# More two by two steps in a fp32 residual block: three up pairs of the second FFN phase and one more gate block

## The chip, the cores and the metric

The kernel runs on one core of a Trainium2 chip. The metric is the device time of one execution in microseconds (us). It is taken in several runs, and one more execution is recorded by the hardware profiler; the page of the profile, its trace and the time of that execution belong together.

## The reference

One residual block on x of 512 tokens by 1024 features, in fp32:

```
h    = rms_norm(x, g1);  proj = h @ w_in          # conv B, C, in | q, k, v | f | gates a, b
y_c  = (B * causal_dwconv3(C * xin)) @ w_out_conv
y_a  = forgetting_attention(q, k, v, f) @ w_out_attn        # 8 heads of 64
x    = x + (sigmoid(ga) * y_c + sigmoid(gb) * y_a) @ w_o
h    = rms_norm(x, g2);  [a | b] = causal_dwconv3(h @ w_up) # 2 x 2816
x    = x + (silu(a) * b) @ w_down
out  = rms_norm(x, gf)
```

## The kernel before

Everything is held transposed: features on the partitions, the 512 tokens along the free axis. A weight block of 128 output features and all 1024 inputs is one chunk (512 KB); the list `stream` names all chunks in the order of use. For a chunk, SyncE (SP) loads `raw`, ScalarE (ACT) rounds it to its high half `wh` (L274), and VectorE (DVE) takes the low half `wl` = raw − wh (L278). Both halves are double buffered, the raws have four buffers (two more kinds for forms, below), and loads run up to seven chunks ahead. The activations are split in the same way (`x1h` and `x1l`, `gh` and `gl`), and a product is three passes: high·high, low·high, high·low (`mm3` L308, `passes` L326). So a chunk's `wl` is wanted by TensorE (PE) only for the last third of its matmuls.

**Two by two steps.** Some products are made in the Strassen-Winograd way: for two blocks of outputs, two of inputs and the two halves of the tokens, seven products take the place of eight. This needs sums of weight blocks and of activation blocks. The sums of weights ("forms") are made in DRAM by DMAs (`make_forms`): plain copies on SP's queue (`put`) and accumulating copies on GpSimd's (POOL) queue (`add`), paced by `slot()`. A double (two products of this kind side by side) comes as two chunks, P (the weights as they are, three blocks) and F (four sums). The sums of activations are made on DVE, by `x_sums` for the gates and by `up_forms` for the up projection; `seven` issues the products; their results are put together from four PSUM banks on DVE and ACT (`gate_pair`, `merge`, `combine`).

**Stages of before (us).** v 0 to 30; q and k to 53; attention with the rest of the input projection to 180; gates, the two branch outputs and their mix, block by block for j = 0 to 7, to 295 (gates from block `GJ` = 3 on in two by two steps); w_o to 339; FFN ups of phase 0 (pairs 0 to 11 of a and b blocks, pairs `SUP` = 1, 2, 5 in steps) to 468; `STEPS[0]`, their down projection in steps, to 525; ups of phase 1 (pairs 12 to 21, all plain) to 634; `STEPS[1]` to 670; a plain rest of the down projection and the final norm.

**What sets the order.** Engines run their instructions in program order. Behind each `split()` the program places small work from the list `later`, up to a budget in us for that chunk (`run_later`); `flush` and `flush_only` empty the list for given tags where a product wants the result. Work tagged "e" is that of the up pairs: `fz` (the PSUM block times the norm), `fu` (three taps of the convolution), then `glu`, which makes silu(a)·b of a pair (`ge`, `go`), and per two pairs q the sums of them (`go`) and the splits into `gh` and `gl`, the operands of the down projection. `HELD` = 2: the sums of output block 2 of the down projection stay in PSUM over phase 1; the others are added to x by `combine` after each phase (`cz`, `cu`).

Of the kernel before, what the change touches and what calls it, by code (L numbers as in the profile page):

```python
# [53 lines left out]
HELD = 2  # L54

GJ = 3
# [14 lines left out]
def block_kernel(ctx, tc, xT, vecs, wv, win, wmix, wo, wup, wst, wdp, outT):  # L71
# [118 lines left out]
    def make_forms(n0, n1, key):  # L190

        size, step, shift = GROUPS[key]
        make_forms.slot = 0
# [4 lines left out]
        for g, (a, b) in enumerate(zip(cuts, cuts[1:])):  # L198
# [15 lines left out]
            todo_bg.extend((make_forms.slot + step * k + shift * g, op) for k, op in enumerate(ops))  # L214
# [167 lines left out]
    ycl = abp.tile([P, 4, S], F32R, tag="ycl", name="ycl")  # L382

# [359 lines left out]

    fill = []
# [41 lines left out]
    def seven(doubles, n0, sets, operand, goes_on=None, stays=None, done=None, of="q"):  # L786
# [14 lines left out]
        for n, (name, prods) in enumerate(todo):  # L801
            wh, wl = chunk(name)
# [4 lines left out]
            for c, i, (xh, xl), b, h in prods:  # L807
                if i not in open_:
# [32 lines left out]
    def mt(name):  # L841
        return mp.tile([P, S], F32, tag="mt", name=name, bufs=6)
# [12 lines left out]
    for q in range(4):  # L855
        nc.gpsimd.dma_start(xt[:, 2 * q : 2 * q + 2, :], xT[:, 2 * q : 2 * q + 2, :])
    xq = xt.rearrange("p (q b) (h c) -> p q (b h) c", b=2, h=2)
    xqh, xql = (t.rearrange("p (q b) (h c) -> p q (b h) c", b=2, h=2) for t in (xth, xtl))

    def x_scale(q):  # L860
        def f():
            for kb in (2 * q, 2 * q + 1):
                nc.scalar.activation(xt[:, kb, :], xt[:, kb, :], AF.Copy, scale=col(G1 + kb))

        return f

    def x_sums(qs):
        b11, b12, b21, b22 = (xq[:, qs, i, :] for i in range(4))

        def f():  # L870
# [637 lines left out]
```

## Time and profile before

| what | value |
|---|---|
| median of 3 runs | 696.37 us (695.74 to 696.41) |
| the profiled execution | 695.75 us, span 693.9 us |
| busy: PE / DVE / ACT / POOL | 686.2 / 531.4 / 359.2 / 178.3 us |
| mean TensorE clock granted | 0.998 |

The span is the time between the first and the last recorded instruction; 1.85 us lie around it. Busy time of PE counts matmuls; weight loads (PEld) run beside them. A row of a timeline has start, duration, engine, line, operation, output<-inputs, and in brackets how long the engine was idle ahead of it and who released it. A row of a group has count, busy time in all, mean ns of one, and the idle time ahead of the group with its releasers. A DMA row has count, KB each and the median us from issue to landing.

### The profile page before, as it was taken

What the parts mean: (1) busy time and instruction counts of PE and PEld (TensorE: products, weight loads), DVE (VectorE), ACT (ScalarE), POOL (GpSimd) and SP (SyncE); (2) the same over time, 40 slices, a digit from 0 to 9 for tenths busy, and PEclk for the clock granted to TensorE, in tenths of its full rate; (3) what the DMA queues carried; (4) which work ended last, traced back from release to release, by engine and by line L of the source; (5) the groups of instructions that cost most, each with busy time, mean ns of one, the idle gap of its engine ahead of it and who ended that gap; (6) DMA issues with size and microseconds to landing.
All of it is one profiled execution on the core that took longest, in us unless ns stands there. A gap on an engine that the chain in (4) does not pass through costs nothing.

```text
span 693.9 us, 14635 instructions
## 1 busy us (share of the span) xinstructions
PE 686.2 (99%) x5972; PEld 684.6 (99%) x5972; DVE 531.4 (77%) x826; ACT 359.2 (52%) x565; POOL 178.3 (26%) x194
## 2 busy tenths in 40 slices
PE   9999999999999999999999999999999999999996
PEld 9999999999999999999999999999999999999996
DVE  6677877776577778768879799888774677777894
ACT  5665655644565444446554455545443344445572
POOL 4134846532221201113513134210000313222000
PEclk9999999999999999999999999999999999999999
DMA  7528988543698596766899776355646686776513
GB/s 256 158 70 272 197 200 193 129 91 92 223 263 244 166 269 193 207 217 141 114 316 294 201 178 135 116 177 176 201 128 232 141 195 157 188 169 172 164 31 122
DMA packets 58387, 124.68 MB, mean 180 GB/s; under 512 B 5280, under 2 KB 26800, under 8 KB 58320
## 3 DMA queue, kind: packets, MB, share of 16 engines
q1 hardware_dynamic: 40776, 99.68, 44.5%
q0 software_dynamic: 16304, 22.88, 20.9%
q10 hardware_dynamic: 1240, 1.19, 0.5%
q8 instruction: 47, 0.77, 0.4%
q14 instruction: 20, 0.16, 0.1%
HBM read 121.57 MB, written 39.32 MB: 232 GB/s over the span
## 4 chain that ended last, share of the span: by engine, by line
PE 96%; DVE 3%; issue 0%; ACT 0%; DVEq 0%
PE dn L326 24%; PE p_up L308 21%; PE p_in L308 14%; PE p_up L326 6%; PE p_wo L308 6%; PE yc L308 3%; PE ya L308 3%; PE pa L472 2%; PE pb L474 2%; PE p_q L308 2%; PE p_k L308 2%; PE p_gb L308 2%; PE p_ga L308 2%; PE o L653 2%; PE tp L636 1%; PE pdB L308 1%
## 5 line engine op out<-in xcount | busy, mean ns | idle before, releaser
L308 PE MATMUL p_up<-x1h,wh_up 128*128 128x256 f32 x464 | 90.5, 276 | 0.0
L308 PE MATMUL p_up<-x1h,wl_up 128*128 128x256 f32 x464 | 90.4, 276 | 0.0
L308 PE MATMUL p_up<-x1l,wh_up 128*128 128x256 f32 x464 | 90.3, 276 | 0.0
L308 PEld LDWEIGHTS p_up<-x1h,wh_up 128*128 128x128 f32 x464 | 69.9, 188 | 0.0
L308 PEld LDWEIGHTS p_up<-x1h,wl_up 128*128 128x128 f32 x464 | 69.9, 188 | 0.0
L308 PEld LDWEIGHTS p_up<-x1l,wh_up 128*128 128x128 f32 x464 | 69.8, 188 | 0.0
L274 ACT ACTIVATE wh_up<-raw_up 128x1024 fp32r<-128x1024 f32 x38 | 40.2, 1057 | 49.6 <-PE p_up L308 43.0
L210 POOL DMA_DIRECT2D f<-in_wst_dram x57 | 65.5, 1309 | 0.1
L278 DVE TENSOR_TENSOR wl_F<-raw_F,wh_F 128x1024 fp32r<-128x1024 f32 (+1 forms) x36 | 47.8, 1328 | 18.5 <-ACT wh_F L274 18.2
L308 PE MATMUL p_in<-xgh,wh_in 128*128 128x256 f32 x288 | 56.8, 279 | 0.0
L308 PE MATMUL p_in<-xgh,wl_in 128*128 128x256 f32 x288 | 56.6, 278 | 0.0
L308 PE MATMUL p_in<-xgl,wh_in 128*128 128x256 f32 x288 | 56.5, 278 | 0.0
L278 DVE TENSOR_TENSOR wl_up<-raw_up,wh_up 128x1024 fp32r<-128x1024 f32 x38 | 47.1, 1240 | 12.1 <-ACT wh_up L274 12.1
L274 ACT ACTIVATE wh_F<-raw_F 128x1024 fp32r<-128x1024 f32 (+1 forms) x36 | 37.9, 1053 | 35.4 <-PE dn L326 27.8
L1206 POOL TENSOR_TENSOR ge<-fu,fu 128x512 f32<-128x512 f32 x11 | 18.8, 1706 | 141.6 <-DVE fu L565 117.6
L274 ACT ACTIVATE wh_P<-raw_P 128x768 fp32r<-128x768 f32 (+1 forms) x36 | 30.0, 834 | 31.6 <-PE dn L326 22.3
L278 DVE TENSOR_TENSOR wl_P<-raw_P,wh_P 128x768 fp32r<-128x768 f32 (+1 forms) x36 | 35.0, 972 | 13.7 <-ACT wh_P L274 9.1
L308 PEld LDWEIGHTS p_in<-xgh,wh_in 128*128 128x128 f32 x288 | 44.7, 188 | 0.7
L326 PE MATMUL dn<-gl,wh_F 128*128 128x256 f32 x192 | 45.1, 276 | 0.0
L326 PE MATMUL dn<-gh,wh_F 128*128 128x256 f32 x192 | 45.1, 276 | 0.0
L308 PEld LDWEIGHTS p_in<-xgl,wh_in 128*128 128x128 f32 x288 | 43.7, 188 | 0.0
L308 PEld LDWEIGHTS p_in<-xgh,wl_in 128*128 128x128 f32 x288 | 43.6, 188 | 0.0
(349 smaller groups left out, 2148.5 us busy)
## 6 DMA issues: line engine op xcount, KB each, us to landing
raw_up<-in_wup_dram SPq DMA_DIRECT2D x38, 512.0 KB, 4.2
raw_F<-f SPq DMA_DIRECT2D x35, 512.0 KB, 4.5
raw_P<-in_wst_dram SPq DMA_DIRECT2D x35, 384.0 KB, 4.9
raw_in<-in_win_dram SPq DMA_DIRECT2D x26, 512.0 KB, 3.5
f<-in_wst_dram POOLq DMA_DIRECT2D x35, 256.0 KB, 6.4
f<-in_wst_dram SPq DMA_DIRECT2D x17, 512.0 KB, 5.7
f<-in_wst_dram POOLq DMA_DIRECT2D x17, 512.0 KB, 8.0
f<-f SPq DMA_DIRECT2D x34, 256.0 KB, 5.4
```

Source lines behind the costliest of these rows:

```text
L210: return lambda: keep(nc.gpsimd.dma_start(dst, src, accum_op=ALU.add))
L274: ins = nc.scalar.activation(hi, raw, AF.Copy)
L278: ins = nc.vector.tensor_sub(lo, raw, hi.bitcast(F32))
L308: keep(nc.tensor.matmul(out[:, cs], w, x[:, cs], start=start and i == 0 and c == 0, stop=stop and i == 2 and c == len(cut) - 1,))
L326: keep(nc.tensor.matmul(out, wl if x == 1 else wh, xl if x == 2 else xh, start=opens and bk not in seen, stop=closes and bk not in left,))
L472: keep(nc.tensor.matmul(pa[t][:, :VW], xt, w[:, VB:], start=start, stop=stop))
L474: keep(nc.tensor.matmul(pb[t], xt, w[:, :VB], start=start and t % 2 == 0, stop=stop and t % 2 == 1))
L636: keep(nc.tensor.transpose(tp[:, ks], pt[:, ks], ident))
L653: keep(nc.tensor.matmul(o[:, 2 * P * e + c0 : 2 * P * (e + 1)], w, x[:, kb, c0:], start=e == 0 and kb == 0 and i == 0, stop=e == 1 and kb ...
L1206: keep(nc.gpsimd.tensor_mul(ge, a.rearrange(halves_of, h=2), b.rearrange(halves_of, h=2)))
```

## The change

- `GJ` goes from 3 to 2: the gates of block 2 are made in steps. `SUP` becomes one tuple for each phase: up pairs 14, 16 and 18 of phase 1 are made in steps too, with forms of their own (`make_forms(..., "up1", 20)`).
- The activation sums of the up projection are needed in both phases. `up_forms(q, ph)` makes them in phase 0 in two buffers by turns (`y` in `gx` or `hp`), and writes each to DRAM (`ys`). In the operand slots 26 to 41 they stand for phase 0; for phase 1 they are read back from `ys` through one buffer `y`, each quarter after the split of the one before, and split into slots 0 to 15, which the down projection of phase 0 has used until then. The first load is issued ahead of `STEPS[0]`, the splits are due at its last chunk and the three after it.
- `HELD` goes: block 2's sums are added to x after both phases, and phase 1 has its PSUM banks. The list `later` is not emptied at the start of phase 1 except of "e" work.
- The x sums for the gates: the loads of `xt` and the scales and sums are moved out of the gate stage. The tile `xt` has memory from the start, so its four loads wait for nothing; the scales and sums are placed in attention. The gates' temporaries use the memory of `x1`, which is loaded in two pieces of 1 MB later.
- In `up`, behind the second block of a phase's last pair: where "e" work is pending, it is flushed, and one more `split()` follows.

The core of the diff (the code of `xt` is only moved, so its removal at the old place is left out):

```diff
@@ -51,20 +51,20 @@
 )
-HELD = 2
-GJ = 3
+GJ = 2
 GATES = tuple(((j, q), (j, q + 1)) for j in range(GJ, KB) for q in (0, 2))
 PLAIN = [(m, k) for m in (6, 7) for k in range(*PHASES[1])]
 PCUTS = (0, 8, 12, 20)
-SUP = (1, 2, 5)
-XF = 26
-UPD = tuple(((j, q), (j, q + 1)) for j in SUP for q in (0, 2))
-DOUBLES = GATES + UPD + STEPS[0] + STEPS[1]
-N0 = len(GATES) + len(UPD)
-GROUPS = {"gate": (2, 4, 1), "up": (2, 4, 1), 0: (2, 4, 1), 1: (2, 3, 1)}
+SUP = ((1, 2, 5), (14, 16, 18))
+XF = (26, 0)
+UPD = tuple(tuple(((j, q), (j, q + 1)) for j in js for q in (0, 2)) for js in SUP)
+DOUBLES = GATES + UPD[0] + STEPS[0] + UPD[1] + STEPS[1]
+NU = [len(GATES), len(GATES + UPD[0] + STEPS[0])]
+ND = [NU[i] + len(UPD[i]) for i in range(2)]
+GROUPS = {"gate": (2, 4, 1), "up0": (2, 4, 1), "up1": (2, 4, 1), 0: (2, 4, 1), 1: (2, 3, 1)}
@@ -187,10 +187,11 @@
-    def make_forms(n0, n1, key):
+    def make_forms(n0, n1, key, start=0):
         size, step, shift = GROUPS[key]
-        make_forms.slot = 0
+        if not start:
+            make_forms.slot = 0
         cuts = [n0]
@@ -211,7 +212,7 @@
             ops = (put(f0, x0), add(f0, x1), put(f1, f[:, :, :m]), add(f1, x1[:, :, m:]), put(f2, f1), add(f2, x2))
-            todo_bg.extend((make_forms.slot + step * k + shift * g, op) for k, op in enumerate(ops))
+            todo_bg.extend((start + step * k + shift * g, op) for k, op in enumerate(ops))
         todo_bg.sort(key=lambda w: w[0])
@@ -381,6 +382,10 @@
+    yg = ExitStack()
+    yp = yg.enter_context(tc.tile_pool(name="yp", bufs=1))
+    xt = yp.tile([P, KB, S], F32, tag="xt", name="xt")
     at = ExitStack()
@@ -740,6 +745,39 @@
     acc, bank_s, bank_t = ring(2, 0, 1), ring(3, 4), ring(5, 6)
+    for q in range(4):
+        nc.gpsimd.dma_start(xt[:, 2 * q : 2 * q + 2, :], xT[:, 2 * q : 2 * q + 2, :])
+    xq = xt.rearrange("p (q b) (h c) -> p q (b h) c", b=2, h=2)
+    def x_scale(q):
+        def f():
+            for kb in (2 * q, 2 * q + 1):
+                nc.scalar.activation(xt[:, kb, :], xt[:, kb, :], AF.Copy, scale=col(G1 + kb))
+        return f
+    def x_sums(qs):
+        b11, b12, b21, b22 = (xq[:, qs, i, :] for i in range(4))
+        def f():
+            nc.vector.tensor_sub(b11, b11, b12)
+            nc.vector.tensor_sub(b12, b22, b12)
+        def g():
+            nc.vector.scalar_tensor_tensor(b22, b11, -1.0, b22, op0=ALU.mult, op1=ALU.subtract)
+            nc.vector.scalar_tensor_tensor(b21, b22, -1.0, b21, op0=ALU.mult, op1=ALU.subtract)
+        return f, g
+    k = len(parts) + 2
+    for q in (0, 2):
+        f, g = x_sums(slice(q, q + 2))
+        for i in (q, q + 1):
+            later.append((k + i - q, 0, (("q", i),), x_scale(i)))
+        later.append((k + 2, 1.4, (("q", q),), f))
+        later.append((k + 3, 1.5, (("q", q),), g))
+        k += 4
@@ -799,6 +837,8 @@
         for n, (name, prods) in enumerate(todo):
+            if tick and name[0] == "P":
+                slot()
             wh, wl = chunk(name)
@@ -811,22 +851,23 @@
                     open_[i][b][:, th[h]], (i, b), wh[:, cs], wl[:, cs], xh, xl,
-                    (i, b) not in before and i != goes_on, (i, b) not in after and i != stays,
+                    (i, b) not in before, (i, b) not in after,
                 ))
             passes(out, len(out))
             if name[0] == "F":
                 for i in sorted({i for _, i, *_ in prods}):
-                    if (i, 0) not in after and i != stays:
+                    if (i, 0) not in after:
                         done(i, open_.pop(i), sets[i])
             split_next()
-    acc = ring(3, 4, 5, 6, 0, 1, 2, 7)
+    acc = ring(3, 4, 5, 6, 2, 7)
     xp = ctx.enter_context(tc.tile_pool(name="xp", bufs=1, side="right"))
-    xt = xp.tile([P, KB, S], F32, tag="x1", name="xt")
+    xm = xp.tile([P, KB, S], F32, tag="x1", name="xm")
     xth = xp.tile([P, KB, S], F32R, tag="x1h", name="xth")
     xtl = xp.tile([P, KB * S + PADR], F32R, tag="x1l", name="xtl")[:, : KB * S]
     xtl = xtl.rearrange("p (a b) -> p a b", b=S)
+    xqh, xql = (t.rearrange("p (q b) (h c) -> p q (b h) c", b=2, h=2) for t in (xth, xtl))
@@ -839,7 +880,10 @@
     def mt(name):
-        return mp.tile([P, S], F32, tag="mt", name=name, bufs=6)
+        mt.n += 1
+        return xm[:, (mt.n + 3) % KB, :]
+    mt.n = 0
@@ -884,16 +903,9 @@
-    k = [c[0] for c in stream].index("mix1")
-    for q in (0, 2):
-        f, g = x_sums(slice(q, q + 2))
-        for i in (q, q + 1):
-            later.append((k, 0, (("q", i),), x_scale(i)))
-        later.append((k, 1.4, (("q", q),), f))
-        later.append((k, 1.5, (("q", q),), g))
-        for i in (q, q + 1):
-            later.append((k + 1, 1.25, (("q", i),), x_split(i)))
-        k += 2
+    k = [c[0] for c in stream].index("mix0")
+    for q in range(4):
+        later.append((k + q // 2, 1.25, (("q", q),), x_split(q)))
@@ -943,15 +955,15 @@
-    make_forms(len(GATES), N0, "up")
+    make_forms(NU[0], ND[0], "up0")
     for j in range(KB):
         gs = []
         for _ in range(3):
             slot()
         if j == KB - 1:
-            x1 = xp.tile([P, KB, S], F32, tag="x1", name="x1")
-            for q in range(4):
-                nc.gpsimd.dma_start(x1[:, 2 * q : 2 * q + 2, :], xT[:, 2 * q : 2 * q + 2, :])
+            assert mt.n == 3 * KB
+            x1 = xm
+            nc.gpsimd.dma_start(x1[:, :4, :], xT[:, :4, :])
         if j == 0:
@@ -960,7 +972,7 @@
             if j == GJ:
-                acc = ring(2, 7, 3, 4)
+                acc = ring(3, 4, 2, 7)
             seven(GATES[2 * (j - GJ) : 2 * (j - GJ) + 2], 2 * (j - GJ), {j: (0, 1, 5, 6)}, gate_form, done=gate_pair(j, gs))
@@ -980,6 +992,8 @@
     mg.close()
+    nc.gpsimd.dma_start(x1[:, 4:, :], xT[:, 4:, :])
+    yg.close()
     ab.close()
@@ -1036,11 +1050,13 @@
-    def up_forms(q):
-        y = gx.tile([P, 4, 2 * P], F32, tag="y", name=f"y{q}")
+    ys = dr.tile([4, P, 4, 2 * P], F32, tag="ys", name="ys")
+    def up_forms(q, ph):
+        y = (gx if ph or q % 2 else hp).tile([P, 4, 2 * P], F32, tag="y", name=f"y{ph}{q}")
         b11, b12, b21, b22 = (y[:, i, :] for i in range(4))
-        fs = slice(XF + 4 * q, XF + 4 * q + 4)
+        fs = slice(XF[ph] + 4 * q, XF[ph] + 4 * q + 4)
@@ -1055,22 +1071,33 @@
         def parts_of():
             nc.scalar.activation(gh[:, fs, :], y, AF.Copy)
+            if not ph:
+                keep(nc.scalar.dma_start(ys[q], y))
             nc.vector.tensor_sub(gl[:, fs, :], y, gh.bitcast(F32)[:, fs, :])
+            if ph and q < 3:
+                up_forms(q + 1, ph)
+        if ph:
+            keep(nc.sync.dma_start(y, ys[q]))
+            due = [c[0] for c in stream].index(f"F{ND[0] + len(STEPS[0]) - 2}") + q
+            later.append((due, 0.85, (("x", q),), parts_of))
+            return
         for f, us in ((scale, 0.85), (sums, 0.85), (parts_of, 1.25)):
             later.append((0, us, (("x", q),), f))
-    def up_form(q, g):
+    def up_form(ph, q, g):
         if g < 3:
             kb, hs = (2 * q, 2 * q + 1, 2 * q + 1)[g], th[(0, 0, 1)[g]]
             return x1h[:, kb, hs], x1l[:, kb, hs]
-        n = XF + 4 * q + (0, 3, 1, 2)[g - 3]
+        n = XF[ph] + 4 * q + (0, 3, 1, 2)[g - 3]
         return gh[:, n, :], gl[:, n, :]
     po = None
-    make_forms(N0, N0 + len(STEPS[0]), 0)
+    make_forms(ND[0], ND[0] + len(STEPS[0]), 0)
+    make_forms(NU[1], ND[1], "up1", 20)
     for j in range(KB):
@@ -1105,11 +1132,11 @@
     acc = turns(0, 1, *(2, 3, 4, 5) * 2, 6, 7, 0, 1, 2, 3, 4, 5)
-    USETS = {1: (2, 3, 4, 5), 2: (6, 7, 0, 1), 5: (6, 7, 0, 1)}
+    USETS = dict.fromkeys(SUP[1], (2, 3, 4, 5)) | {1: (2, 3, 4, 5), 2: (6, 7, 0, 1), 5: (6, 7, 0, 1)}
     ssq3 = xp.tile([P, S], F32, tag="ssq", name="ssq3")
     def place(ph, q):
-        return (q - PHASES[ph][0] // 2) * (NF + ph)
+        return (16, 24, 32, 0, 8)[q - PHASES[1][0] // 2] if ph else q * NF
@@ -1134,6 +1161,9 @@
                 split_next()
+                if any(("e",) in w[2] for w in later):
+                    flush_only((("e",),))
+                    split()
             z = [None]
@@ -1292,10 +1322,8 @@
         if ph:
-            flush()
-            acc = turns(*X * 5)
-        if ph:
-            make_forms(N0 + len(STEPS[0]), len(DOUBLES), ph)
+            acc = turns(6, 7, 0, 1, 6, 7, 0, 1, 6, 7, 0, 1, 6, 7)
+            make_forms(ND[1], len(DOUBLES), ph)
         for j in range(j0, j1):
@@ -1309,14 +1337,15 @@
             up(j, ph, nrm["b"], pu)
+        if not ph:
+            up_forms(0, 1)
+        flush_only((("e",),))
+        seven(
+            STEPS[ph], ND[ph], ({0: X, 1: Y, 3: X, 2: Y}, {0: X, 1: Y, 2: Y})[ph],
+            lambda q, g: (gh[:, place(ph, q) + g, :], gl[:, place(ph, q) + g, :]),
+            done=lambda i, banks, ids: combine(ph, i, banks, ids), tick=True,
+        )
         assert not todo_bg
-        flush((("e",),))
-        seven(
-            STEPS[ph], N0 + ph * len(STEPS[0]), ({0: X, 1: Y, 3: X, 2: Y}, {0: X, 1: Y, 2: Y})[ph],
-            lambda q, g: (gh[:, place(ph, q) + g, :], gl[:, place(ph, q) + g, :]),
-            goes_on=HELD if ph == 1 else None, stays=HELD if ph == 0 else None,
-            done=lambda i, banks, ids: combine(ph, i, banks, ids),
-        )
```

**Where the order moves, POOL at the start.** The loads of `xt` on GpSimd's queue; `kb` and `qb` are the memsets of attention's operands, `rc_n` a step of the first norm. Before, the memsets run on into `rc_n`, and the loads stand at the end of attention:

```order
L527 MEMSET kb_111 4x512
L526 MEMSET kb_112 64x512
L527 MEMSET kb_112 4x512
L355 TENSOR_TENSOR rc_n_415<-ms_n_413,ex 128x4
L694 MEMSET fo 32x512
```

After:

```order
L531 MEMSET kb_116 64x512
L750 DMA xt<-in_xT_dram 128x1024
L532 MEMSET kb_116 4x512
L750 DMA xt<-in_xT_dram 128x1024 x3
L356 TENSOR_TENSOR rc_n_419<-ms_n_417,ex 128x4
L699 MEMSET fo 32x512
```

One load stands ahead of the last memset and three behind it, with no wait.

**DVE at the start of phase 1.** `wl_F` and `wl_P` are the last chunks of `STEPS[0]`, the first `wl_up` is that of up block 24, `cz`, `cu` and `x` (after: `xm`) belong to `combine`, `gl<-y` is the split of a read-back quarter. Before:

```order
L278 TENSOR_TENSOR wl_F_6799<-raw_F_6591,wh_F_6798 128x1024
L1271 TENSOR_TENSOR x_3803<-x_3803,cu_6745 128x512
L278 TENSOR_TENSOR wl_P_6828<-raw_P_6619,wh_P_6827 128x768
L278 TENSOR_TENSOR wl_F_6852<-raw_F_6652,wh_F_6851 128x1024
L278 TENSOR_TENSOR wl_up_6880<-raw_up_6678,wh_up_6879 128x1024
L278 TENSOR_TENSOR wl_up_6948<-raw_up_6739,wh_up_6947 128x1024
L1141 TENSOR_TENSOR fz_6938<-p_up_6889,rb_n_4669 128x512
```

After:

```order
L279 TENSOR_TENSOR wl_F_6818<-raw_F_6607,wh_F_6817 128x1024
L1079 TENSOR_TENSOR gl<-y_6192,gh 128x1024
L279 TENSOR_TENSOR wl_P_6850<-raw_P_6635,wh_P_6849 128x768
L1301 TENSOR_TENSOR xm<-xm,cu_6763 128x512
L279 TENSOR_TENSOR wl_F_6879<-raw_F_6668,wh_F_6878 128x1024
L1079 TENSOR_TENSOR gl<-y_6823,gh 128x1024
L279 TENSOR_TENSOR wl_up_6911<-raw_up_6695,wh_up_6910 128x1024
L279 TENSOR_TENSOR wl_up_6986<-raw_up_6757,wh_up_6985 128x1024
L1283 TENSOR_TENSOR cz_6916<-dn_6737,cz_6916 128x256
L1286 TENSOR_TENSOR xm<-dn_6735,xm 128x512
L1079 TENSOR_TENSOR gl<-y_6884,gh 128x1024
```

Two splits of y now stand ahead of the first `wl_up`, a third behind the second one, and the sums of block 2 are put together there.

**DVE at the start of the last steps.** `fz211` and `fu211` are of the last up block (pair 21), `go9` and `gl` the sums and splits of pairs 18 and 19, `go10` those of pairs 20 and 21, and P28, F28, P29 (after: P36, F36, P37) the first chunks of `STEPS[1]`. Before:

```order
L1141 TENSOR_TENSOR fz211_8215<-p_up43_8158,rb_n2_4669 128x512
L278 TENSOR_TENSOR wl_F28_8245<-raw_F28_8009,wh_F28_8244 128x1024
L562 SCALAR_TENSOR_TENSOR fu211_8217<-fz211_8215,vec_64,fu211_8217 128x511
L278 TENSOR_TENSOR wl_P29_8275<-raw_P29_8078,wh_P29_8274 128x768
L565 SCALAR_TENSOR_TENSOR fu211_8217<-fz211_8215,vec_64,fu211_8217 128x510
L278 TENSOR_TENSOR wl_F29_8299<-raw_F29_8080,wh_F29_8298 128x1024
L1213 TENSOR_TENSOR go10_8223<-fu210_8141,fu211_8217 128x512
```

After:

```order
L1171 TENSOR_TENSOR fz211_8284<-p_up43_8206,rb_n2_4668 128x512
L279 TENSOR_TENSOR wl_F36_8279<-raw_F36_8049,wh_F36_8278 128x1024
L1253 TENSOR_TENSOR go9_8196<-ge9_7995 128x256
L1254 TENSOR_TENSOR go9_8196<-go9_8196,ge9_7995 128x256
L567 SCALAR_TENSOR_TENSOR fu211_8286<-fz211_8284,vec_64,fu211_8286 128x511
L1257 SCALAR_TENSOR_TENSOR go9_8196<-go9_8196 128x256
L570 SCALAR_TENSOR_TENSOR fu211_8286<-fz211_8284,vec_64,fu211_8286 128x510
L1258 SCALAR_TENSOR_TENSOR go9_8196<-go9_8196 128x256
L1263 TENSOR_TENSOR gl_3989<-ge9_7995,gh_3988 128x2x256
L1263 TENSOR_TENSOR gl_3989<-go9_8196,gh_3988 128x512 x3
L279 TENSOR_TENSOR wl_P37_8352<-raw_P37_8115,wh_P37_8351 128x768
```

All of `go9` and its `gl`, which stood ahead of P28 before, now lie between the second and the third chunk.

More of the change, by code (lines that the diff above doesn't have):

```diff
@@ L784, in block_kernel, with seven @@
     open_ = {}
-    def seven(doubles, n0, sets, operand, goes_on=None, stays=None, done=None, of="q"):
+    def seven(doubles, n0, sets, operand, done=None, of="q", tick=False):
         todo, wants = [], {}
@@ L851, in evac_gate @@
         return f
-    for q in range(4):
[L856 to L870, printed above, removed]
-            nc.vector.tensor_sub(b11, b11, b12)
-            nc.vector.tensor_sub(b12, b22, b12)
-        def g():
-            nc.vector.scalar_tensor_tensor(b22, b11, -1.0, b22, op0=ALU.mult, op1=ALU.subtract)
-            nc.vector.scalar_tensor_tensor(b21, b22, -1.0, b21, op0=ALU.mult, op1=ALU.subtract)
-        return f, g
     def x_split(q):
@@ L1086, in block_kernel @@
         if j % 2:
-            up_forms(j // 2)
+            up_forms(j // 2, 0)
     hg.close()
@@ L1120, in tap @@
             uu.append(u)
-        if j in SUP:
-            c = len(GATES) + 2 * SUP.index(j)
+        if j in SUP[ph]:
+            c = 2 * SUP[ph].index(j)
             slot()
             seven(
-                UPD[c - len(GATES) :][:2], c, {j: USETS[j]}, up_form, of="x",
+                UPD[ph][c : c + 2], NU[ph] + c, {j: USETS[j]}, lambda q, g: up_form(ph, q, g), of="x",
                 done=lambda i, banks, ids: merge(ph, j, banks, ids, rb2, tap, uu),
@@ L1461, in _layout @@
     wu4 = wup.reshape(2 * NP, P, KB, P)
-    for w4, d in [(wga, d) for d in GATES] + [(wu4, d) for d in UPD] + [(wdn, d) for d in STEPS[0] + STEPS[1]]:
+    for w4, d in [(wga, d) for d in GATES] + [(wu4, d) for d in UPD[0]] + [(wdn, d) for d in STEPS[0]] + [(wu4, d) for d in UPD[1]] + [(wdn, d) for d in STEPS[1]]:
         def pick(*which):
```

3 lines of the change are left out of this document (1 added, 2 removed).

## The prediction

> **What bounds the kernel now.** I began with the head of the page: the busy time of each engine, then the chain that ended last.
>
> ```profile
> span 693.9 us, 14635 instructions
> PE 686.2 (99%) x5972; PEld 684.6 (99%) x5972; DVE 531.4 (77%) x826; ACT 359.2 (52%) x565; POOL 178.3 (26%) x194
> PE 96%; DVE 3%; issue 0%; ACT 0%; DVEq 0%
> ```
>
> TensorE (PE) is busy for 99% of the span and is 96% of the chain. So matmuls that go are worth their whole time, and everything else counts only where it makes PE wait. The chain in order of time gives the price of a matmul in the four places where the change works (start, time, group, count):
>
> ```profile
> 187.72 5.44 PE p_ga L308 x48
> 193.16 5.44 PE p_gb L308 x48
> 220.36 9.52 PE dn L326 x84
> 468.15 57.12 PE dn L326 x504
> ```
>
> 48 matmuls take 5.44 us, 84 take 9.52, 504 take 57.12: 113.3 ns each, plain or in two by two steps. The first two rows are the gates of block 2, plain, 96 matmuls and 10.88 us; the third is the gates of block 3, in steps. Then I asked how full VectorE (DVE) is by stage, since it makes the low halves of every weight chunk and all sums. The columns are PE, PEld, DVE, ACT and POOL busy, the granted clock, the DMA share and GB/s; the rows are attention, the ups of phase 0, two pieces of them, and the ups of phase 1.
>
> ```profile
> 53.00:180.00 127.00, 127.00 (x1083) 126.31 (x1083) 92.67 (x209) 68.89 (x155) 61.59 (x75) 1.00 0.67 163
> 339.00:468.00 129.00, 128.37 (x1131) 128.09 (x1130) 111.47 (x162) 67.42 (x95) 36.95 (x29) 1.00 0.73 197
> 414.00:430.00 16.00, 15.37 (x135) 15.17 (x134) 16.00 (x28) 8.79 (x14) 7.25 (x5) 1.00 0.49 118
> 430.00:450.00 20.00, 20.00 (x179) 20.00 (x178) 18.03 (x28) 10.89 (x16) 4.85 (x2) 1.00 0.49 135
> 525.00:634.00 109.00, 109.00 (x964) 109.00 (x963) 77.95 (x109) 48.03 (x67) 27.09 (x24) 1.00 0.72 177
> ```
>
> The clock is full throughout. PE waits at one place: in 414 to 430 DVE is busy all 16 us and PE loses 0.6. That is among the up pairs that are in steps already; phase 1, all plain, has DVE at 77.95 of 109.
>
> **The matmuls: −5.44 us.** Gates of block 2 and up pairs 14, 16, 18 go from 96 matmuls to 84 each: 4 × 12 = 48, × 113.3 ns = −5.44. Nothing on PE is added: block 2's down sums are only closed and opened again. The order shows PE with 5937 matmuls before and 5889 after, so it does what it says.
>
> **xt at the start: +1.5 us.** The four loads of xt (512 KB each, 2.1 MB) move from 185.6 us to the memsets at the head of POOL's queue; ahead of them nothing is waited for. POOL reaches them at 9.6. The loads of v's weights are then in flight. The rows are in turn: the memset behind which three of them stand, SP's issue of the last four v chunks, ScalarE's (ACT) work on the first of these, PE's first matmul with it, and the engines' DMA load in 12 to 14 us.
>
> ```profile
> 9.63 0.52 POOL L527 MEMSET kb<- 4x512 f32 x1
> 9.18 3.91 SPq L182 DMA_DIRECT2D raw_v<-in_wv_dram  x4
> raw_v<-in_wv_dram SPq DMA_DIRECT2D x4, 260.0 KB, 4.9
> 14.22 0.64 ACT L274 ACTIVATE wh_v<-raw_v 128x520 fp32r<-128x520 f32 x1 [0.57 <-PE pb L474]
> 14.77 0.71 ACT L453 ACTIVATE xgh<-xs,vec 128x512 fp32r<-128x512 f32 x1
> 16.89 0.28 PE L472 MATMUL pa<-wh_v,xgh 128*128 128x264 f32 x1
> 12.00:14.00 2.00, 2.00 (x19) 2.00 (x18) 1.97 (x3) 1.65 (x3) 0.00 (x0) 1.00 1.07 383
> ```
>
> The chunk issued at 9.18 lands at about 9.18 + 4.9 = 14.1; ACT splits it at 14.22, goes on to xgh until 15.48, and PE wants both at 16.89. So it may come 0.14 + 1.41 = 1.55 us later for nothing. DMA is full there (share 1.07), so bytes that get in between cost time. How much is not in the trace; the nearest rows are what SP's loads took while the same xt loads ran at 186 to 200 us (first three rows), against their usual landing (last two, whole run):
>
> ```profile
> xt<-in_xT_dram POOLq DMA_DIRECT2D x4, 512.0 KB, 5.4
> raw_F<-f SPq DMA_DIRECT2D x1, 512.0 KB, 8.2
> raw_P<-in_wst_dram SPq DMA_DIRECT2D x1, 384.0 KB, 7.4
> raw_F<-f SPq DMA_DIRECT2D x35, 512.0 KB, 4.5
> raw_P<-in_wst_dram SPq DMA_DIRECT2D x35, 384.0 KB, 4.9
> ```
>
> They landed 3.7 and 2.5 us late, 3.1 in the mean; less 1.55, PE waits 1.5. Bounds: 0 if the xt packets start too late to matter; if all 2.1 MB go first at 393 GB/s (10 to 12 us shows about that, the row above 383), 2.1 MB / 0.39 = 5.4 late, 3.8 of wait. A gain is excluded, since nothing at the start is taken away. The later v chunks are wanted some 3 us apart and land 0.7 apart, so the wait comes once. [...] The gate stage loses these transfers, but PE waited nowhere there, so that gains nothing.
>
> **x sums in attention, gates of block 2: 0.** The sums are 8 DVE operations and 8 ACT scales, put between attention's chunks: in the gate stage of before such a sum takes 0.69 us and a scale 0.71. The window 53 to 180 above has PE without a gap, DVE at 73% and ACT at 54%, so 5.6 us more on each, in pieces, find room. What hides a piece is the lead that the weight chunks and transposes have over PE; without it each would cost its 0.7, 5.6 at the most if none had any. The gates of block 2 get the load that blocks 3 to 7 have without a wait.
>
> **y read back at the start of phase 1: +0.2 us.** Pairs 14 to 18 need the x sums of phase 0 in the operand slots again: four loads of 512 KB through one buffer, each split by ACT (gh) and DVE (gl), each load only after the split before. Two of these splits stand on DVE's queue ahead of the low half of the first up chunk.
>
> ```profile
> raw_up<-in_wup_dram SPq DMA_DIRECT2D x6, 512.0 KB, 3.6
> raw_up<-in_wup_dram SPq DMA_DIRECT2D x38, 512.0 KB, 4.2
> L1059 ACT ACTIVATE gh<-y 128x1024 fp32r<-128x1024 f32 x4 | 4.2, 1061 | 8.0 <-DVE y L1056 8.0
> L1060 DVE TENSOR_TENSOR gl<-y,gh 128x1024 fp32r<-128x1024 f32 x4 | 4.9, 1226 | 4.6 <-ACT gh L1059 4.6
> 515.98 1.23 DVE L278 TENSOR_TENSOR wl_F<-raw_F,wh_F 128x1024 fp32r<-128x1024 f32 x1 [0.41 <-ACT wh_F L274]
> 523.00 1.23 DVE L278 TENSOR_TENSOR wl_up<-raw_up,wh_up 128x1024 fp32r<-128x1024 f32 x1 [1.04 <-ACT wh_up L274]
> 526.02 0.39 PE L326 MATMUL p_up<-x1h,wl_up 128*128 128x256 f32 x2
> ```
>
> The wl_F of 515.98 ends at 517.2; the split of the first y behind it ends at 518.4, and only then is the second y loaded. With 3.6 us (the loads of this size in 500 to 532 us) it lands at 522.0, gh to 523.1, gl to 524.3, wl_up to 525.5: in time for 526.02. With 4.2 it is 0.1 late; with the 5.4 that xt's loads of that size took, 1.3, and part of it again at the next split. I take 0.2, between the first two, with 0 and 2.0 as ends. What the y loads write (ys, by ACT's queue at 295 to 339) has 130 us.
>
> **DVE's queue at the start of the last steps: +2.4 us.** The placed work of phase 1 falls behind. The eight sums and splits (go, gl) of the hidden pairs 18 and 19, which stood inside phase 1 before, now stand between a wl_F and the wl_P of the next double, as the order shows, with two steps (fu) of the last block among them.
>
> ```profile
> 635.28 1.23 DVE L278 TENSOR_TENSOR wl_F<-raw_F,wh_F 128x1024 fp32r<-128x1024 f32 x1 [0.47 <-ACT wh_F L274]
> 637.08 0.95 DVE L278 TENSOR_TENSOR wl_P<-raw_P,wh_P 128x768 fp32r<-128x768 f32 x1
> 636.42 0.74 DVE L562 SCALAR_TENSOR_TENSOR fu<-fz,vec,fu 128x511 f32<-128x511 f32 x1
> 641.99 0.42 DVE L1223 TENSOR_TENSOR go<-ge 128x256 f32<-128x256 f32 x1
> L1233 DVE TENSOR_TENSOR gl<-go,gh 128x512 fp32r<-128x512 f32 x33 | 22.4, 698 | 0.0
> 640.03 0.50 PE L326 MATMUL dn<-gh,wl_P 128*128 128x256 f32 x3
> ```
>
> The wl_F starts at 635.28 as before, since it waits for the last up block's end. Then by these rows: wl_F 1.23, four go at 0.42, two fu at 0.74, four gl at 0.70, wl_P 0.95: 8.1 us. Neighbours in such runs start about 0.08 sooner than the one ahead ends (636.42 − 635.28 is 1.14 for the 1.23), so 11 × 0.08 = 0.9 goes: 7.2, end at 642.5. PE wants this wl_P at 640.03: 2.4 of wait. Ends: 3.1 without most of the overlap, 1.7 if a go or gl fits into the 0.47 idle. After it the next wl_F comes 1.1 later against 24 matmuls, so no second wait.
>
> **Sum.** −5.44 + 1.5 + 0.2 + 2.4 = −1.3. The profiled execution took 695.75 (span 693.9 and 1.85 around it): 694.4 after. The median of the runs is 696.37, 0.6 above it: **695.0**.
>
> **Rivals.** *The waits mostly don't come* (xt's bytes fall behind those of v, y is in time): −5.44 + 2.4 = −3.0, 693.3; if DVE also has its queue empty in time for the last steps, −5.44, 690.9. For it: POOL's loads may be slow to start, and only 4.0 us of the v chunk are left at 10.1. Against: DMA at 1.07 exactly there, and the order of the last steps is fixed. *xt goes all first*: 3.8 for 1.5, +1.0, 697.4. Against it: in the gate stage SP's loads came late, but not behind all of xt.
>
> *Slower: DVE bounds phase 1.* The work there grows. A pair in steps has two P and two F splits for two plain ones, and seven merges in place of two fz:
>
> ```profile
> L278 DVE TENSOR_TENSOR wl_F<-raw_F,wh_F 128x1024 fp32r<-128x1024 f32 x35 | 47.1, 1346 | 17.8 <-ACT wh_F L274 17.6 <-ACT uz L1162 0.2
> L278 DVE TENSOR_TENSOR wl_up<-raw_up,wh_up 128x1024 fp32r<-128x1024 f32 x38 | 47.1, 1240 | 12.1 <-ACT wh_up L274 12.1
> L1141 DVE TENSOR_TENSOR fz<-p_up,rb_n 128x512 f32<-128x512 f32 x38 | 25.9, 686 | 18.7 <-PE p_up L308 18.7
> ```
>
> Splits 2 × (1.35 + 0.95, the wl_P above) − 2 × 1.24 = 2.1, merges at most 7 × 0.69 − 2 × 0.69 = 3.4, three times: 16.6. With four gl of y (4.9) and the sums of block 2 now closed after phase 0 (seven operations, at most 4.8): 77.95 + 26.3 = 104.3, in 109 − 3 × 1.36 = 104.9 us of matmuls. That is full, as in 414 to 430, where only 0.6 was lost in 16. In 430 to 450 DVE stood at 90% with PE full. If gaps and waits let it fill no more than 95%, phase 1 takes 109.8, 4.9 more: −5.44 + 1.5 + 0.2 + 2.4 + 4.9 = +3.6, 699.9. It decides from the point at which DVE's merges run later than the four PSUM banks of the next pair are wanted. Against it: the 104.3 is an upper end (half of the merges are 256 columns wide), and the seven plain pairs between have air.
>
> **How the numbers follow.** The forecast with its own ends gets 0.50: its sum lies at the edge of what a measurement of this kernel can tell, 0.2% or 1.4 us, so 0.21 of it counts as faster and 0.29 as the same. Waits that don't come: 0.24, faster. xt first: 0.08, the same. DVE bound: 0.18, slower. Faster 0.45, same 0.37, slower 0.18. Range: downward to half way between 693.3 and 690.9 (692.1), upward past xt's worst (697.4), half way to the DVE case's 699.9 (698.6).
>
> **What would show it.** Right: 5.44 less in PE's matmul time; one PE gap of about 1.5 at 16 to 18 us behind wh_v; one of 2.4 at 636 to 642 (shifted) behind wl_P; DVE near 95% in phase 1. Wrong: no gap at the start while raw_v lands as before; several gaps in phase 1 behind wl_up or behind merges; gaps in attention behind transposes.

## Result and profile after

The changed kernel is slower by 0.7%: 701.41 us, median of 4 runs (699.37 to 702.24), against 696.08 before in the same comparison; the ratio is 1.0074, 95% interval [1.0062, 1.0085]. A second comparison of the same kernel gave 701.21 (700.21 to 703.34) and 1.0076 [1.0062, 1.0089]. Forecast were 695.0 and a range up to 698.6. The profiled execution took 699.37, 3.6 more than that of before.

The head of the page after: PE has less work than before (682.9 for 686.2), and the span is longer.

```profile
span 697.6 us, 14699 instructions
PE 682.9 (98%) x5924; PEld 680.0 (97%) x5924; DVE 556.9 (80%) x865; ACT 371.2 (53%) x582; POOL 192.7 (28%) x204
```

Three starts on PE divide the change: the first matmul of `STEPS[0]`, the first of `STEPS[1]` (both of the timeline), and the plain rest (of the chain).

```profile
467.87 0.28 PE L327 MATMUL dn<-gh,wh_P 128*128 128x256 f32 x1
630.36 0.28 PE L327 MATMUL dn<-gh,wh_P 128*128 128x256 f32 x1
673.04 6.80 PE pdA L309 x60
```

Before, the first two stood at 468.15 and 634.07, and the third at 634.07 + 35.91 = 669.98. Up to the first: −0.3, which is −1.36 for the gates and +1.1 of waiting. From there to the second: −3.4, which is −4.08 for the three pairs and +0.65. The last steps take 42.68 us for 35.91: +6.8. Behind them another 0.6. In all +3.7. So the matmuls went as forecast, and some 9 us came on top: 8.5 us of waits of PE, most of them in one place, and 0.6 behind them. The view of PE's waits names what ended last (us in all, times, longest):

```profile
PE dn L327 <- ACT wh_P L275: 2.4, 2, 1.5
PE dn L327 <- DVE gl L1263: 1.6, 2, 1.4
PE dn L327 <- ACT wh_F L275: 1.5, 1, 1.5
PE p_up L327 <- DVE wl_up L279: 0.6, 1, 0.6
PE dn L327 <- DVE wl_P L279: 0.5, 1, 0.5
PE dn L327 <- DVE wl_F L279: 0.4, 1, 0.4
```

Of these only the wl_up row was there before. In the timeline these are, in order, a wait in pair 2 of phase 0, one in pair 14, and four of the five at the start of the last steps; the fifth, the 1.4 us for a split gl of go10, ends at 652.4:

```profile
365.50 0.38 PE L327 MATMUL dn<-x1h,wh_P 128*128 128x256 f32 x1 [0.94 <-ACT wh_P L275]
555.88 0.38 PE L327 MATMUL dn<-x1h,wl_F 128*128 128x256 f32 x1 [0.35 <-DVE wl_F L279]
634.04 0.38 PE L327 MATMUL dn<-gh,wh_F 128*128 128x256 f32 x1 [1.47 <-ACT wh_F L275]
638.55 0.39 PE L327 MATMUL dn<-gh,wh_P 128*128 128x256 f32 x1 [1.51 <-ACT wh_P L275]
640.37 0.38 PE L327 MATMUL dn<-gl,wh_P 128*128 128x256 f32 x1 [0.25 <-DVE gl L1263]
641.23 0.95 PE L327 MATMUL dn<-gh,wl_P 128*128 128x256 f32 x6 [0.48 <-DVE wl_P L279]
```

Each costs some 0.3 us more than its bracket, since PE's ends are modelled and run past the next start (in the rows a matmul has 0.28 us, and the next starts 0.11 behind its start): counted from start to start the seven are 8.5 us.

How the first two at the last steps come about, in DVE's, POOL's and ACT's rows:

```profile
629.69 1.84 DVE L567 SCALAR_TENSOR_TENSOR fu<-fz,vec,fu 128x511 f32<-128x511 f32 x1
634.02 1.22 DVE L279 TENSOR_TENSOR wl_F<-raw_F,wh_F 128x1024 fp32r<-128x1024 f32 x1 [1.10 <-ACT wh_F L275]
629.70 1.29 POOL L1236 TENSOR_TENSOR ge<-fu,fu 128x512 f32<-128x512 f32 x1 [4.26 <-ACT fu L566]
632.41 0.63 ACT L1231 ACTIVATE fu<-fu 128x512 f32<-128x512 f32 x1 [2.75 <-DVE fu L570]
632.95 1.04 ACT L275 ACTIVATE wh_F<-raw_F 128x1024 fp32r<-128x1024 f32 x1
634.62 1.28 ACT L1233 ACT_TABLE_LOAD   x1
636.64 1.13 ACT L1262 ACTIVATE gh<-go 128x512 fp32r<-128x512 f32 x2
637.67 0.83 ACT L275 ACTIVATE wh_P<-raw_P 128x768 fp32r<-128x768 f32 x1
```

DVE is behind with its taps, and the one of 629.69 (first block of the last pair) takes 1.84 us for 0.74 while POOL makes `ge` of the pair ahead. ACT stands 2.75 us in front of the silu of that block, and the chunk split wh_F is queued behind the silu, so that wl_F is late too. The wh_P of 637.67 then stands behind the splits of pairs 18 and 19 (gh), and these behind a table load of 1.28 with a small operation of 0.29 that belongs to it; the program places both behind the silu of the last pair. ACT has no gap from 632.41 to the end of this wh_P, so up to 1.6 us of its lateness are theirs. Before, the same load stood at 632.70 ahead of a wh_F that PE did not wait for. No run here moves it.

### The profile page after: what moved, and what is told of

Read it like the earlier page. It is cut to its first block, busy times and chain, and to the rows that moved or that the text cites. A ratio compares the mean times of both kernels' runs of the same rounds, so it can differ in the third digit from the quotient of the medians.

```text
span 697.6 us, 14699 instructions
## 1 busy us (share of the span) xinstructions
PE 682.9 (98%) x5924; PEld 680.0 (97%) x5924; DVE 556.9 (80%) x865; ACT 371.2 (53%) x582; POOL 192.7 (28%) x204
## 5 line engine op out<-in xcount | busy, mean ns | idle before, releaser
L211 POOL DMA_DIRECT2D f<-in_wst_dram x69 | 80.4, 1420 | 36.1 <-DMA f<-f 35.7
L309 PE MATMUL p_up<-x1h,wl_up 128*128 128x256 f32 x392 | 76.4, 276 | 0.0
L309 PE MATMUL p_up<-x1h,wh_up 128*128 128x256 f32 x392 | 76.4, 276 | 0.0
L309 PE MATMUL p_up<-x1l,wh_up 128*128 128x256 f32 x392 | 76.3, 276 | 0.0
L279 DVE TENSOR_TENSOR wl_F<-raw_F,wh_F 128x1024 fp32r<-128x1024 f32 (+1 forms) x44 | 58.4, 1326 | 21.9 <-ACT wh_F L275 21.7
L309 PEld LDWEIGHTS p_up<-x1h,wl_up 128*128 128x128 f32 x392 | 59.1, 188 | 0.0
L309 PEld LDWEIGHTS p_up<-x1l,wh_up 128*128 128x128 f32 x392 | 59.0, 188 | 0.0
L309 PEld LDWEIGHTS p_up<-x1h,wh_up 128*128 128x128 f32 x392 | 59.0, 188 | 0.0
L327 PE MATMUL dn<-gh,wh_F 128*128 128x256 f32 x228 | 54.0, 277 | 1.5 <-ACT wh_F L275 1.5
L327 PEld LDWEIGHTS dn<-gh,wh_F 128*128 128x128 f32 x228 | 42.8, 188 | 1.7 <-ACT wh_F L275 1.7
```

Of the source, the lines that this page charges most:

```text
L211: return lambda: keep(nc.gpsimd.dma_start(dst, src, accum_op=ALU.add))
L279: ins = nc.vector.tensor_sub(lo, raw, hi.bitcast(F32))
L309: keep(nc.tensor.matmul(out[:, cs], w, x[:, cs], start=start and i == 0 and c == 0, stop=stop and i == 2 and c == len(cut) - 1,))
L327: keep(nc.tensor.matmul(out, wl if x == 1 else wh, xl if x == 2 else xh, start=opens and bk not in seen, stop=closes and bk not in left,))
```

## Experiments

All are edits of the changed kernel, timed in five rounds beside the kernel before, which took 695.9 in each of the three comparisons.

**The changed kernel again.**

> The changed kernel once more, unchanged, to see which of its waits stand in another execution. The theory from its first trace: 8.5 us of PE waits, in three groups: 1.2 us in pair 2 of phase 0 (the raw_P load, held up beside the ys writes), 0.6 in pair 14, and 6.6 at the start of the last steps (DVE's and ACT's queues behind). If these are the whole cause, the same gaps come again within 0.3 us each and the time is 700 to 702. The rival (waits that come from the chance of the DMAs' timing): other gaps in other places, of 1 us and more.

701.21, 1.0076. The waits at the last steps come again, each within 0.05 us:

```profile
365.93 0.38 PE L327 MATMUL dn<-x1h,wh_P 128*128 128x256 f32 x1 [1.38 <-ACT wh_P L275]
634.70 0.39 PE L327 MATMUL dn<-gh,wh_F 128*128 128x256 f32 x1 [1.48 <-ACT wh_F L275]
639.21 0.38 PE L327 MATMUL dn<-gh,wh_P 128*128 128x256 f32 x1 [1.51 <-ACT wh_P L275]
```

So they come from the order of the queues. The one in pair 2 is 0.4 longer, more than the 0.3 that was expected: it hangs on a transfer.

The executions of this kernel lie 3 us apart (700.21 to 703.34). Each of the three single edits below that helped gains about 2 us in the median, and its interval just meets this one at 1.0062; what makes these gains firm is that they add up when the edits are joined.

**The last ys write later.**

```diff
-            if not ph:
+            if q == 3 and not ph:
+                due = [c[0] for c in stream].index("up18")
+                later.append((due, 0, (), lambda: keep(nc.scalar.dma_start(ys[q], y))))
+            elif not ph:
                 keep(nc.scalar.dma_start(ys[q], y))
```

> The changed kernel; only the last of the four ys writes (512 KB) is issued later, at up block 18 (about 440 us) in place of 343.5. Theory A: this write delays the raw_P load of pair 2, so the gap of 1.2 us at 364 goes and nothing else changes: 1.2 less, about 700.2. Rival (PE comes 1.4 us sooner to a load that is late by itself): the gap stays above 0.8.

699.28 (698.82 to 701.03), 1.0050 [1.0038, 1.0062]: 1.9 less than the control. The gap at 364 is gone in the profile, the others stand. The DMA rows of 337 to 367 us, first of the changed kernel, then of this one:

```profile
raw_P<-in_wst_dram SPq DMA_DIRECT2D x3, 384.0 KB, 11.1
ys<-y ACTq DMA_DIRECT2D x1, 512.0 KB, 11.0
```

```profile
raw_P<-in_wst_dram SPq DMA_DIRECT2D x3, 384.0 KB, 9.8
```

With the write, a raw_P took 11.1 us in the median; without it 9.8. The one that PE waits for is the last of the three: issued at 349.46 it took 15.0 us with the write, issued at 348.44 it took 14.5 without (before: issued at 348.73, 13.4). A wait in pair 2 stands in all five profiles that have the write at its old place (two of them of the changed kernel), where this load lands at 364.5 to 366.1, and in two of the seven that have it late, where it lands at 362.5 to 365.4: the write makes it later, but it is close to late without it. The wait that went is 1.2 to 1.7 us from start to start, so the 1.9 of the medians is not accounted for to the last tenths.

**No emptying ahead of the last split.**

```diff
-                if any(("e",) in w[2] for w in later):
-                    flush_only((("e",),))
-                    split()
```

> The changed kernel without the emptying of the list ahead of the last split of each phase (the three lines in up). The list is emptied one chunk later then, so that more of it stands in front of the F chunk and less in front of the P chunk. Theory A: the same work is late by the same amount; the gaps shift between F36, P37 and P39, their sum stays within 1.5 us of 6.6, and the time is 700 to 703. Rival (the emptying itself causes the waits): the sum of the gaps falls below 3, time about 697.5.

698.93 (696.64 to 701.73), 1.0048 [1.0033, 1.0062]: 2.3 less, which the rival expected and my theory did not. wh_F now stands on ACT ahead of that silu, and one long wait is left of five at the last steps. It is for a wl_F behind go9 and its splits on DVE:

```profile
638.12 1.21 PE L327 MATMUL dn<-gh,wl_F 128*128 128x256 f32 x8 [2.54 <-DVE wl_F L279]
```

**Both together.**

> Both single steps that helped: the last ys write at up block 18, and no emptying ahead of the last split. If their causes are separate their gains add: 701.2 - 1.9 - 2.3 = 697.0. If they are one (PE just comes sooner into the next wait): 698.5 or more.

696.79, 1.0011 [1.0003, 1.0020]: the two gains add (701.21 − 1.93 − 2.28 = 697.0).

**Larger budgets in phase 1.**

```diff
-            run_later(k, {"u": 4.2, "P": 1.6, "F": 1.2}[nm[0]])
+            run_later(k, ({"u": 5.6, "P": 2.3, "F": 2.1} if len(parts) > PH1 else {"u": 4.2, "P": 1.6, "F": 1.2})[nm[0]])
```

> The changed kernel; only the budgets of the small work placed behind each split are larger from up block 26 on (5.6, 2.3, 2.1 us for up, P and F chunks in place of 4.2, 1.6, 1.2). Same instructions and matmuls; the sums and splits of pairs 18 and 19 stand inside phase 1 again. Theory A (the budgets put the work off until it lands in front of the last steps' chunks): the gaps of 1.7, 1.8, 1.3 and 1.7 us at 632 to 651 go, PE waits there less than 1 us, and the time falls by 5 to 6.5, to about 695.5. Theory B (DVE has no room in phase 1): the waits come back inside phase 1 behind wl_up and wl_F, and the time stays at 700 to 702.

703.27, 1.0110 [1.0094, 1.0126]. Theory A falls: go9 stands inside phase 1 as before, and three waits came there, in pairs 16 and 18 (0.95 to 1.82 us), two of them in the same form (a silu waits for DVE, and wh_F stands behind it). One of 1.96 us for a wh_F is left at the last steps, at 642.84; this wh_F stands behind the late silu and, directly, behind the table load (640.25 to 641.75 with its small operation). A row of PE, and two windows behind it; the clock is the third column from the end:

```profile
573.39 0.38 PE L328 MATMUL dn<-x1h,wh_F 128*128 128x256 f32 x1 [1.82 <-ACT wh_F L276]
571.00:575.00 4.00, 2.18 (x15) 1.98 (x14) 2.90 (x4) 3.24 (x5) 0.00 (x0) 0.85 0.79 242
575.00:580.00 5.00, 5.00 (x36) 5.00 (x36) 3.81 (x9) 2.43 (x4) 3.61 (x4) 0.78 0.35 96
```

**The products on DVE.** In phase 1 `ge` and `go` are made by `nc.vector`, not `nc.gpsimd`.

> The changed kernel; only the products silu(a) * b of phase 1 (ge, go) are made on DVE, not on GpSimd. Theory C (beside these GpSimd products a DVE instruction takes 0.7 to 1.1 us longer, and DVE also waits for them): nine products at some 0.6 us each are paid for by the stretching that goes, pair 14's gap of 0.6 goes, and the late silu ahead of wh_F comes sooner: the sum of the gaps falls by 1 to 2, to 699.5. Rival (DVE is simply full): 5 us more work on it, gaps grow, 702.5 or more.

699.50, 1.0045 [1.0031, 1.0059]: 1.7 less, although DVE has nine instructions more. The wait in pair 14 and the one at 634 are gone; the one for wh_P at the last steps is longer, and the matmuls behind it run slow. It is no longer DVE that holds this wh_P: the silu at 632.68 comes without a wait, and up to wh_P at 637.55 ACT works without a gap, on the table load (1.28 us at 633.97) and the four splits of pairs 18 and 19 (2.3 us) among others. The row of PE and two windows:

```profile
638.43 0.53 PE L327 MATMUL dn<-gh,wh_P 128*128 128x256 f32 x1 [2.21 <-ACT wh_P L275]
636.00:638.40 2.40, 0.22 (x2) 0.02 (x1) 2.40 (x5) 2.40 (x6) 0.00 (x0) 1.00 0.41 164
638.40:641.70 3.30, 3.27 (x15) 3.27 (x16) 2.99 (x4) 1.29 (x2) 0.00 (x0) 0.52 0.08 20
```

**The gates alone.** `SUP = ((1, 2, 5), ())`, and no ys.

> The changed kernel with no up pair of phase 1 in steps (all ten plain), and without the writing and reading back of y: what is left is the gates of block 2 in steps, xt loaded at the start, x sums in attention, and block 2's down sums closed after each phase. Theory (the loss sits in the three up pairs and in the ys writes): 12 matmuls less, 1.36 us, and 0 to 0.7 at the start: 694.6 to 695.3 against 695.9 before, no gap over 0.3 us but the old one at 419. Rival (xt at the start or the gates themselves cost): 696.5 and more, with a gap before 30 us or in 180 to 295.

694.71, 0.9981 [0.9972, 0.9990]: faster by 1.2 with 12 matmuls (1.36 us) less. So the gates, xt at the start, the x sums in attention and block 2's sums cost 0.2 together by the medians, at most 0.7 by the interval. The profile has one wait of PE more than before, 0.78 us at 5.5 us, but that is ahead of the first load of xt, which is issued at 9.52. (Here and in the three edits below that have two pairs or other pairs in steps, the turns in which phase 1's plain blocks take the PSUM banks are set to fit.)

**Two pairs, late ys write.** `SUP = ((1, 2, 5), (14, 16))`.

> The changed kernel with up pair 18 plain again (14 and 16 in steps) and the last ys write at up block 18. Theory A (pair 18 leaves too little time to work off DVE's queue before the last steps): the four gaps at 632 to 651 go, as does the one at 364; left is the 0.6 in pair 14: 36 matmuls less, 4.08 us, so 695.9 - 4.1 + 0.6 + 0.4 = 692.8. Theory B (DVE has no room for any step pair in phase 1): gaps of 2 us and more stay inside phase 1 or at its end: 695 or more.

695.15, 0.9988 [0.9979, 0.9997]: a miss by 2.4. The long waits at the last steps are gone, but shorter ones stand at 555, 610 and 634.

**Two pairs, late ys write, products on DVE.**

> Pairs 14 and 16 in steps, the last ys write late, and phase 1's products ge and go on DVE: the candidate for a kernel that beats both. In the run before it (with the products on GpSimd) PE waited 0.6 in pair 14, 0.7 at 610 behind a wl_up that took 2.3 us beside a GpSimd product, and 0.8 at 633. Theory C: all three come from the stretching beside GpSimd, and go: 695.15 - 2 = 693.1. Rival (the added 10 products on DVE push other work back): 695 or more.

692.11 (691.90 to 692.47), 0.9940 [0.9928, 0.9952]: faster than both kernels (by 0.6% than the kernel before), and 1.0 us less than theory C expected. PE has no gap in phase 1, nor at the last steps. Phase 1:

```profile
520.00:629.00 109.00, 109.00 (x964) 109.00 (x963) 98.06 (x144) 55.99 (x76) 14.38 (x15) 1.00 0.77 215
```

**All three pairs with everything.** Without the emptying ("alldv") and with the larger budgets ("budall"):

> All three pairs in steps, with the late ys write, without the emptying, and with the products on DVE. If the three causes are separate: 701.2 - 1.9 - 2.3 - 1.7 = 695.3. Theory B (with three pairs DVE has no room, whatever is placed where): one wait of 2 us and more is left at the start of the last steps, 696 to 697.

> All three pairs in steps, the late ys write, the products on DVE, and the larger budgets. The larger budgets alone cost 2 us, since in pairs 16 and 18 the silu on ACT, in front of wh_F, waited for a DVE that was behind; DVE was held up there by GpSimd's products. If that stretching was what held it up, the waits at 571, 596 and 603 go, those at the start of the last steps stay away: 692 to 694. If DVE is full either way: 697 or more.

695.31, 0.9983 [0.9972, 0.9994], and 694.93, 0.9983 [0.9974, 0.9992]. The median of the first is what the three single gains add up to (695.3); that it agrees so closely is luck, since its executions lie between 693.55 and 696.78. Its profile, of the longest of them, still has the one long wait at the last steps that theory B expected, and one in pair 2:

```profile
PE dn L327 <- DVE wl_F L279: 2.0, 1, 2.0
PE dn L327 <- ACT wh_P L275: 1.4, 1, 1.4
```

In budall neither is there, but PE waits in phase 1, where DVE is busy for 99.2 of 108 us. Its time lies between the two that were expected (692 to 694, and 697 or more):

```profile
PE p_up L328 <- DVE wl_up L280: 1.5, 2, 0.9
PE dn L328 <- DVE wl_P L280: 0.9, 1, 0.9
520.00:628.00 108.00, 106.16 (x919) 104.96 (x918) 99.20 (x148) 55.72 (x77) 14.44 (x15) 1.00 0.79 222
```

**Pairs 13 and 15.**

> As the two-pair candidate, but pairs 13 and 15 in steps in place of 14 and 16, so that DVE has two chunks more to work its queue off, and y has to be there 11 us sooner. If the time after the last pair in steps is what counts: as the candidate or up to 0.5 better. If y's chain of four loads is now late (the last split of y ended at 536): a gap of 1 us and more in pair 13, 694 to 696.

694.48, 0.9982 [0.9969, 0.9995]: the second case. One wait is left that the two-pair candidate has not, in pair 13. The last quarter of y comes late: ACT's half of the split waits 1.70 us for the load, and DVE stands idle for ACT's half. Behind it on DVE is the sum `xm` of `combine`, which reads the PSUM banks that the pair wants next; PE's wait ends with it:

```profile
534.25 1.23 DVE L1082 TENSOR_TENSOR gl<-y,gh 128x1024 fp32r<-128x1024 f32 x1 [1.70 <-ACT gh L1076]
536.06 0.68 DVE L1297 TENSOR_TENSOR xm<-xm,dn 128x512 f32<-128x512 f32 x1
536.79 0.38 PE L327 MATMUL dn<-gh,wh_P 128*128 128x256 f32 x1 [1.33 <-DVE xm L1297]
```

## Why the prediction was wrong

Added up by the stretches above, the change is −5.44 + 1.1 (pair 2) + 0.65 (pair 14) + 6.8 (last steps) + 0.6 (behind them) = +3.7 us, where −5.44 + 1.5 + 0.2 + 2.4 = −1.3 was forecast.

**The matmuls (−5.44): right.** Up to the last steps the time falls by what they save, less 1.75 of waits. (The two rows shown ahead for the gates of block 2 are those of block 1; block 2's stand at 204.04 and 209.48 and take the same 5.44.)

**xt at the start (+1.5): wrong, 0.** The collision is there: in 9 to 30 us the last v chunks land in 6.5 us in the median, where they took 4.9. The estimate took its delay from 186 to 200 us for the chunk that is wanted first. That chunk, issued at 9.30, took 5.4 us and landed at 14.7, 0.6 later than before, inside the 1.55 that were to spare; the next two, which took 6.5 and 8.1, are wanted later, and ACT splits the last three chunks within 0.02 us of where it did.

```profile
raw_v<-in_wv_dram SPq DMA_DIRECT2D x4, 260.0 KB, 6.5
xt<-in_xT_dram POOLq DMA_DIRECT2D x4, 512.0 KB, 9.1
```

**x sums, gates (0): right**, shown by the gates alone.

**y at the start of phase 1 (+0.2): right, 0.** The step-by-step times hold: second y there for ACT at 521.5 (forecast 522.0), first wl_up from 523.7.

```profile
521.50 1.06 ACT L1076 ACTIVATE gh<-y 128x1024 fp32r<-128x1024 f32 x1 [0.91 <-DMA y<-ys]
523.74 1.22 DVE L279 TENSOR_TENSOR wl_up<-raw_up,wh_up 128x1024 fp32r<-128x1024 f32 x1
```

**What was left out: the ys writes (1.2 to 1.9).** I checked that they are in time for their readers, and not what queues beside them. The last one goes out at 343.5, not by 339 as I had it, where phase 0's first chunks are loaded and DMA is full (its share is 1.03 from 343 to 367).

**The last steps (+2.4): the place right, the size wrong, 6.8.** The term was the one wait for wl_P behind go9. At that point PE waits 1.51 + 0.25 + 0.48, 3.2 from start to start, which is not far from 2.4, but most of it is for ACT's wh_P. The step that failed is "the wl_F starts at 635.28 as before, since it waits for the last up block's end". It starts 3.7 us behind the first P chunk on PE, not 1.2, since DVE comes to it late and ACT's wh_F is queued behind a silu that waits for DVE; for this wh_F PE waits 1.6 us from start to start that no term had. And behind go9 the same lack of time returns at go10 (1.8 from start to start), against "so no second wait". I followed DVE's order there but not ACT's, on which the table load and the splits of pairs 18 and 19 stand ahead of wh_P.

**The rival "DVE bounds phase 1" (0.18, 699.9) came nearest, by another path.** That DVE has too little room is borne out from three sides: with larger budgets waits come inside phase 1; with two pairs and the products off GpSimd those of phase 1 and of the last steps vanish; with three pairs some stay in every version tried. But it is not the whole cause: the late ys write and the missing emptying took 1.9 and 2.3 us away without taking work off DVE. And the path was another: the rival had merges come too late for the PSUM banks of the next pair, and in the changed kernel no wait of PE stands behind a merge; they stand behind splits. Its place was off too: the work was put off to the end of the phase, so that 520 to 630 shows DVE at 96.7 of 110 us, 88% and not 95%, and little wait:

```profile
520.00:630.30 110.30, 109.95 (x970) 109.75 (x969) 96.67 (x133) 55.95 (x75) 28.85 (x24) 1.00 0.79 224
```
 
The 104.3 I worked out as an upper end leaves out how much longer DVE's operations took beside GpSimd's products: a tap 1.49 us and one 1.84 for 0.74, and a wl_up 2.3 for 1.2:

```profile
609.90 2.32 DVE L279 TENSOR_TENSOR wl_up<-raw_up,wh_up 128x1024 fp32r<-128x1024 f32 x1 [0.21 <-ACT wh_up L275]
609.83 1.29 POOL L1236 TENSOR_TENSOR ge<-fu,fu 128x512 f32<-128x512 f32 x1 [3.23 <-DVE fu L570]
```

The wl_up starts just behind the product and lasts longer by 1.1, nearly all of the product's 1.29; how the one holds up the other is not shown. With the products on DVE, in the two-pair kernel, the `wl_up` of the whole run take 1.24 us in the mean and the taps with 511 columns of plain blocks 0.77, where the changed kernel has 1.28 and 0.82. Beside operations that read PSUM a product cost DVE nothing here: the `go` at 602.2 ran beside `uz`, `ua` and `uu` (0.42, 0.69 and 0.41 us, no longer than elsewhere).

**Open.** The 0.6 us behind the last steps lie among the final stores: from the end of DVE's last instruction to the end of the span it is 3.45 us before and 4.1 after, and between 3.5 and 4.3 in the profiles of the experiments, with the same stores; it was not followed further. How much of the wait for wh_P the table load makes was not measured. Nor is it shown why an execution of the changed kernel takes 699 or 703. Three things differ from profile to profile of these kernels: the wait in pair 2 (none to 1.9 us), a wait of 0.2 to 0.8 us at 5 to 9 us, ahead of the loads of xt, which six of the profiles have, and the clock, to which the section on the hardware comes.

## What to carry to other kernels

Where an engine makes operands just in time, count its work in the stretch that the change fills, with what a product on the engine beside it adds (here 1.1 us to a wl_up of 1.2), before counting matmuls: the third pair in steps saved 1.36 us of PE, and the best kernel with it is 2.8 us slower than the best with two (694.93 for 692.11; the two differ in their budgets too). Follow every in-order queue at the tight place, not only the busiest: here ACT was 53% busy and held the chunk that PE waited for. A transfer that nobody waits for can still have a price where DMA is full: the one write moved here, out of a stretch with a DMA share of 1.03, gave 1.9 us.

## What the runs showed of the hardware

Some waits of PE cost more than their length, others did not. In the kernel with the products on DVE the granted clock was 0.52 for 3.3 us behind an idle time of 2.2 (15 matmuls where 29 fit). With larger budgets it was 0.78 from 575 to 580, behind one of 1.8, but 1.00 from 642 to 648, behind one of 1.96. Behind the waits of 1.5 us in both profiles of the changed kernel it stayed at 1.00. And the same wait of 2.54 us for wl_F, with the same rows around it, was followed by full clock in the kernel without the emptying (1.00 from 638 to 640), and by half clock in that with the late write added (0.50 in the same 2 us; eight matmuls take 2.08 us, where the row of 638.12 above has 1.21):

```profile
637.75 2.08 PE L327 MATMUL dn<-gh,wl_F 128*128 128x256 f32 x8 [2.54 <-DVE wl_F L279]
```

What sets the clock behind a wait is not shown; the length of the wait alone does not, with 0.52 behind one of 2.2 us and 1.00 behind one of 2.54. So the spread from 700.2 to 703.3 of the changed kernel may come in part from this, at each of its waits: the two longest executions, 702.22 and 703.34, have the lowest granted clocks, 0.994 and 0.991. It is not all of it, since 701.65 has 0.998 like 700.29. This was not tested.
